# State-space scan at every fourth time in one sequence over all tiles, layer-1 keys behind the first output product, a one-array gate operand

## The chip, the cores and the metric

The kernel runs on one core of a Trainium2 chip. TensorE (PE) multiplies matrices, VectorE (DVE), ScalarE (ACT) and GpSimd (POOL) work on elements, and SyncE (SP) issues almost all DMA transfers; each engine takes its instructions in the order in which they were written. The metric is device time of one execution in microseconds (us).

## What is computed

Two decoder layers on 256 positions of width 4096. Each layer multiplies the normalised input by one wide matrix, runs a recurrent branch (a state-space model in layer 0, a gated linear recurrence in layer 1), attends to a fixed memory, gates both and multiplies by an output matrix.

```python
for i in range(2):
    hn = rmsnorm(h, pre_norm[i])
    u, gate, q, q_gate = split(hn @ w_in[i], [3072, 6144, 7168])
    y = s5_mixer(u, ...) if i == 0 else rglru_mixer(u, ...)
    m = memory_attention(q, rmsnorm(mem, mem_norm[i]), w_kv[i])   # k and v are mem_n @ w_kv
    h = h + rmsnorm(concat[y * silu(gate), m * silu(q_gate)] @ w_out[i], post_norm[i])

def s5_mixer(u, ...):      # 192 groups of 16 channels, 64 complex states each
    x = einsum(u, Bbar)                      # input of each state
    s[t] = Abar * s[t-1] + x[t]              # diagonal recurrence over 256 times
    y = gelu(re(einsum(s, C)) + d * u)
    return y * sigmoid(y @ w_glu + b_glu)
```

## The kernel before, in words

Activations lie with channels on the partitions and the 256 times along the free dimension. Every product splits its float32 operands in two parts, hi and lo: ACT rounds a weight piece to hi (L126), DVE subtracts to get lo (L90), and PE multiplies hi by both parts of the activation and lo by its hi part (L130). `add_phase` cuts each matrix into steps of one 512 KB weight piece, eight blocks of 128 by 128. There are 980 steps: u0 (96 steps), g0 (96), gq0, q0, k0, v0 and k1 (32 each) and glu (72), then out0 (128), v1 (32), u1 (96), gq1, q1, g1 with 12 gate steps, and out1. In form "w2" a block takes two matmuls, one of 512 columns and one of 256, in forms "n2", "n4" and "n8" three of 256.

`run` (L421) writes the program step by step. In a step come first the pieces of work that are due (`at`, `hook`), then the matmuls of the step, the split of the piece two steps ahead, then side work (`run_side`: generators that go on while a count of DVE and ACT time lies behind that of PE), and last the DMA of the piece five steps ahead into one of three `raw` buffers (`load_w`). All DMAs of `self.dma` (L134) go to the one SP queue, so a piece of side work stands in it between two weight pieces. The DMAs use eight completion semaphores in turn, and a DMA waits for the one issued eight before it.

The state-space branch `s5` is side work. `s5_a_b` forms the input coefficients and stores them in DRAM (`bD`). `x_load` (L818) fetches a tile's coefficients and two phases (even and odd times) of u, `x_mm` multiplies them, and the state input goes to a big buffer X. That buffer holds 48 of the 96 state tiles, so the branch runs in two blocks of 12 channel tiles: load, then 127 sequential scan steps of one DVE multiply and two adds, then the output stage. In that stage `y_coef` (L854) makes coefficients on POOL, `d0_mm` and `y_mm` multiply on PE, and DVE and ACT apply the GELU. The result goes to DRAM, rounded and remainder apart (`gHL`), and is read back as the operand of glu. A glu step may only be written when its tiles are done (`ready`); until then the steps written are without matmuls of weights.

`boundary` (L553) forms layer 1's input between out0 and u1, in 16 chunks c: f0 (a DVE multiply, then a DMA issued by POOL that adds x into the chunk `bh`), f1 two steps later (ACT writes `Bhn`, rounded) and f2 one step after (DVE writes the remainder).

Of the kernel before, what the change touches and what calls it, by code (L numbers as in the profile page):

```python
# [20 lines left out]
T = 256  # L21
# [7 lines left out]
BT = 48  # L29
TH = T // 2  # L30
# [15 lines left out]
def blocks(nm, form=None, n=0):  # L46
# [4 lines left out]
         "k0": blocks(KX, "n4", 4), "v0": [(0, KX, "v")], "k1": blocks(KX, "n4", 4),  # L51
         "glu": blocks(KE, "n4", 4), "out0": blocks(KD), "v1": [(0, KX, "v")],
         "u1": blocks(KE, "n4", 8), "gq1": blocks(KX), "q1": blocks(KX), "g1": blocks(KE), "out1": blocks(KD)}
# [9 lines left out]
class Trunk:  # L63
# [84 lines left out]
    def setup(self):  # L148
# [404 lines left out]
    def boundary(self):  # L553
        self.B = self.big.tile([128, 2, KD, T], F32R, name="Bhn", tag="B")
        rb = self.rbx.unsqueeze(1).to_broadcast([128, 2, T])
        for c in range(KD // 2):
# [32 lines left out]
            w = self.step + 1 + 2 * c  # L589
# [138 lines left out]

    def s5(self):
# [36 lines left out]
        yield  # L766
        self.mul(t0, nr, lr)
# [9 lines left out]
        self.mul(t0, kr, ar)  # L777
        self.mul(t1, nki, ai)
        self.add(k2r, t0, t1)
        self.mul(t0, nki, ar)  # L780
        self.mul(t1, kr, ai)
        self.sub(nk2i, t0, t1)
        yield
        self.mul(t0, ar, ar)
        self.mul(t1, ai, ai)
        self.sub(A2[:, :, 0, 0], t0, t1)
        self.sub(A2[:, :, 1, 1], t0, t1)
        yield
        self.mul(t0, ar, ai)
        self.ts(A2[:, :, 0, 1], t0, 2.0, ALU.mult)  # L790
        self.ts(A2[:, :, 1, 0], t0, -2.0, ALU.mult)
        d0s = [sp.tile([128, 128], F32, name=f"d0{i}", tag=f"d0{i}", bufs=1) for i in range(2)]
        W = [sp.tile([128, 1024], F32, name=f"W{i}", tag=f"W{i}", bufs=1) for i in range(2)] + [tail(2560, 1024)]
        W = [w.rearrange("p (i j c q) -> p i j c q", i=2, j=2, c=2) for w in W]
        for t in d0s + W:
            self.nc.gpsimd.memset(t, 0.0)
        yield
        asb = X0[:, 12288:12544].rearrange("p (k q) -> p k q", k=2)
        ps = self.ps_x.tile([128, 2, T], F32, name="psa", tag="x")
        for k in range(2):  # L800
            self.pe_t += 214
            self.nc.tensor.transpose(ps[:, k, 0:128], cf[:, 128 * k:128 * k + 128], self.ident)
        self.acopy(asb, ps[:, :, 0:128])
        yield "wait"
        for k, n, rows in ((0, 0, asb[0:NT, 0]), (1, 0, asb[NT:128, 0]), (1, 128 - NT, asb[0:2 * NT - 128, 1])):
            self.dma(self.aD[n:n + rows.shape[0], :, k], rows.rearrange("n (g q) -> n g q", g=2))
        yield "wait"
# [4 lines left out]
        self.ab = deque(self.s5_a_b(tail(0, 3072), 12, 6) + self.s5_a_b(tail(0, 3072), 18, 6))  # L812
        self.nc.gpsimd.memset(X[:, :, :, 0:1], 0.0)

        st = {}


        def x_load(ct, w, u):  # L818
# [10 lines left out]
        def x_mm(blk, ct):  # L829
            w, u, _ = st.pop(("x", ct))  # L830
            for i in range(2):
                ps = self.ps_x.tile([128, 2, 2, TH], F32, name="psx", tag="x")
                for j in range(2):
                    for c in range(2):
                        self.mm(ps[:, j, c, :], w[:, i, j, c, :], u[:, i, :], True, True, 218)
                n = 4 * ct - blk * BT + 2 * i
                self.acopy(X[:, n:n + 2, :, 1:], ps)


        v4 = lambda t: t.rearrange("p (c j m) -> p c j m", c=2, j=4)  # L840

        def y_load(ct, part):
            s = st.setdefault(ct, {})
            if part == 0:
                s["craw"] = v4(tail(1536 + 256 * (ct % 2), 256))
                self.dma(s["craw"], I["s5c"][ct])
            elif part == 1:
                s["b2"] = v4(tail(2048 + 256 * (ct % 2), 256))
                self.dma(s["b2"], I["s5b2"][ct])
            else:  # L850
                s["u"] = sp.tile([128, T], F32, name="u", tag="u")
                self.dma(s["u"], self.uF[ct])

        def y_coef(ct):  # L854
            s = st[ct]
            P = v4(tail(3584, 256))
            Q = v4(sp.tile([128, 256], F32, name="cQ", tag="cQ", bufs=1))
            g = self.nc.gpsimd
            for i, (re, im) in enumerate(((kr, nki), (k2r, nk2i))):
                C = v4(tail(2560 + 512 * (ct % 2) + 256 * i, 256))  # L860
                b = lambda v: v[:, 4 * ct:4 * ct + 4].unsqueeze(1).unsqueeze(3).to_broadcast([128, 2, 4, 32])
# [4 lines left out]
                s["C", i] = C  # L866

        def d0_mm(ct):
            s = st[ct]
            d = self.pm[:, 0, 0:32]  # L870
            for k in range(2):
                for j in range(4):
                    self.mm(d[32 * j:32 * j + 32], s["b2"][:, k, j, :], s["C", 0][:, k, j, :], k == 0, k == 1, 66)

        def d0_copy(ct):
            d = d0s[ct % 2]
            for j in range(4):
                r = slice(32 * j, 32 * j + 32)
                self.acopy(d[r, r], self.pm[r, 0, 0:32])

        def y_mm(blk, ct):
            s = st[ct]
            c = ct - blk * (BT // 4)
            ps = self.pm[:, 1, :].rearrange("p (e t) -> p e t", e=2)
            s["y"] = ps
            self.done.add(("ym", ct))
            ue = s["u"][:, 0:TH]
            self.mm(ps[:, 0, :], d0s[ct % 2], ue, True, False, 218)
            for e in range(2):
                for k in range(2):  # L890
                    for j in range(4):
                        self.mm(ps[32 * j:32 * j + 32, e, :], s["C", 1 - e][:, k, j, :],
                                X[:, c * 4 + j, k, e:e + TH], e == 1 and k == 0, k == 1, 74)

        def y_tasks(blk, ct, S):
# [25 lines left out]
            at(S - 5, lambda: y_load(ct, 0))
            at(S - 4, lambda: y_load(ct, 1))
            at(S - 2, lambda: y_coef(ct))
            at(S, lambda: y_load(ct, 2))
            at(S, lambda: d0_mm(ct))
            at(S + 1, lambda: d0_copy(ct))
            at(S + 2, lambda: y_mm(blk, ct))
# [484 lines left out]
```

## Time and profile before

| what | value |
|---|---|
| median of 3 runs | 3048.28 us (3039.66 to 3050.7) |
| profiled execution | 3042.13 us, of which the span from first to last instruction is 3040.4 us |
| PE busy | 2923.2 us, 96% of the span |
| DVE, ACT, POOL busy | 2084.3, 1586.9, 165.4 us |
| mean granted TensorE clock | 0.98 of full speed |

"Busy" is time in which an engine had an instruction running. Matmuls overlap one another, so their mean duration is longer than the distance from one to the next, and a row's count divided by its window gives the pace. A granted clock of 1.00 is 2.4 GHz, 0.50 is 1.2 GHz. Names left of an arrow are written, those right of it read.

### The profile page before, as it was taken

The numbers are of one execution on the slowest core, as the hardware profiler recorded it, in microseconds if no ns is written. First come the engines' busy times: TensorE is split into PE (matmuls) and PEld (weight loads), VectorE is DVE, ScalarE is ACT, GpSimd is POOL, SyncE is SP. The second block draws the span as 40 slices with busy tenths as digits, with TensorE's granted clock in tenths as the row PEclk, the third lists the DMA queues.
The fourth block names the chain that finished last, engine by engine and source line by source line (L and its number), as shares of the span: only waits on it lengthen the run. The fifth ranks groups of instructions, "written<-read, shape, count | busy, mean of one in ns | idle before, by whom it ended". The sixth has DMA issues, their size and how long they took to land.

```text
span 3040.4 us, 52558 instructions
## 1 busy us (share of the span) xinstructions
PE 2923.2 (96%) x18318; PEld 2582.6 (85%) x18318; DVE 2084.3 (69%) x4597; ACT 1586.9 (52%) x3073; POOL 165.4 (5%) x225
## 2 busy tenths in 40 slices
PE   9999999999999977999999998999999999999996
PEld 9998888888998976888888876988888888888885
DVE  8739989668999853565655555678888766655555
ACT  6444444454655443555655554456666555455553
POOL 1000000340000052000000001000000000000001
PEclk9999999999999987999999999999999999999998
DMA  8777666776767775656766689666667566666664
GB/s 273 217 215 223 199 197 201 214 228 207 244 214 233 217 237 184 211 188 215 239 208 198 202 237 242 196 211 216 214 209 218 188 217 196 198 205 202 200 205 156
DMA packets 286347, 644.12 MB, mean 212 GB/s; under 512 B 38912, under 2 KB 158976, under 8 KB 285824
## 3 DMA queue, kind: packets, MB, share of 16 engines
q1 hardware_dynamic: 279872, 634.72, 66.9%
q0 software_dynamic: 4352, 4.20, 0.9%
q8 instruction: 144, 2.36, 0.3%
q10 hardware_dynamic: 1856, 1.84, 0.2%
q14 instruction: 123, 1.01, 0.1%
HBM read 592.81 MB, written 47.81 MB: 211 GB/s over the span
## 4 chain that ended last, share of the span: by engine, by line
PE 80%; DMA 8%; DVE 6%; issue 2%; ACT 2%; SPq 1%; ACTq 0%; DVEq 0%; POOLq 0%
PE acc L130 76%; DVE lo L90 3%; DMA st<-gF 1%; PE pm L130 1%; DMA gHL<-gh 1%; PE psg L130 1%; PE psx L130 1%; ACT hi L126 1%; SPq L134 1%; DMA bh<-in_x 1%; DVE e L90 1%; DMA u<-uF 1%; DVE Bs L90 1%; DMA bo<-og 1%; DVE Bfin L90 0%
## 5 line engine op out<-in xcount | busy, mean ns | idle before, releaser
L90 DVE TENSOR_TENSOR lo<-raw,hi 128x512 fp32r<-128x512 f32 (+1 forms) x2434 | 1341.2, 587 | 773.3 <-ACT hi L126 734.5
L126 ACT CAST hi<-raw 128x512 fp32r<-128x512 f32 x1960 | 1139.9, 618 | 771.7 <-PE acc L130 358.4
L130 PE MATMUL acc<-A,hi 128*128 128x512 f32 (+1 forms) x4896 | 1494.6, 367 | 37.5 <-DMA A<-gHL 21.5
L130 PE MATMUL acc<-A,lo 128*128 128x256 f32 x4160 | 1175.5, 283 | 2.9 <-DVE lo L90 2.8
L130 PEld LDWEIGHTS acc<-A,hi 128*128 128x128 f32 x4896 | 886.1, 192 | 196.3 <-DMA A<-gHL 20.8
L130 PEld LDWEIGHTS acc<-A,lo 128*128 128x128 f32 x4160 | 796.0, 191 | 10.7 <-DVE lo L90 10.1
L130 PE MATMUL acc<-Bhn,hi 128*128 128x512 f32 (+1 forms) x2304 | 726.4, 373 | 13.2 <-ACT hi L126 13.2
L130 PE MATMUL acc<-Bhn,lo 128*128 128x256 f32 x2048 | 576.2, 281 | 2.5 <-DVE lo L90 2.5
L130 PEld LDWEIGHTS acc<-Bhn,hi 128*128 128x128 f32 x2304 | 419.7, 190 | 92.4 <-ACT hi L126 15.4
L130 PEld LDWEIGHTS acc<-Bhn,lo 128*128 128x128 f32 x2048 | 389.9, 190 | 5.8 <-DVE lo L90 5.5
L130 PE MATMUL acc<-Bmix,hi 128*128 128x512 f32 x1024 | 355.6, 391 | 0.4 <-ACT hi L126 0.4
L130 PE MATMUL acc<-Bmix,lo 128*128 128x256 f32 x1024 | 287.0, 280 | 0.2 <-DVE lo L90 0.2
L130 PEld LDWEIGHTS acc<-Bmix,hi 128*128 128x128 f32 x1024 | 191.5, 187 | 42.9 <-ACT hi L126 0.7
L130 PEld LDWEIGHTS acc<-Bmix,lo 128*128 128x128 f32 x1024 | 193.5, 189 | 0.8 <-DVE lo L90 0.8
L130 PE MATMUL acc<-hi,A 128*128 128x512 f32 x512 | 160.5, 395 | 12.6 <-ACT hi L126 12.6
L90 DVE TENSOR_TENSOR Bs<-Bs,m 128x96 f32<-128x96 f32 x508 | 168.3, 331 | 2.9
L130 PEld LDWEIGHTS acc<-hi,A 128*128 128x128 f32 x512 | 97.0, 191 | 34.2 <-ACT hi L126 14.3
L126 ACT COPY e<-acc 128x256 f32<-128x256 f32 x200 | 73.5, 368 | 75.6 <-PE acc L130 74.7
L130 PE MATMUL acc<-lo,A 128*128 128x512 f32 x256 | 101.4, 396 | 0.0
L122 ACT ACTIVATE e<-e 128x256 f32<-128x256 f32 x64 | 26.7, 418 | 138.2 <-DVE e L90 138.0
L90 DVE TENSOR_TENSOR m<-A,Bs 128x192 f32<-128x192 f32 x254 | 90.4, 356 | 8.9 <-ACT Bs L126 3.5
L90 DVE TENSOR_TENSOR e<-e,acc 128x256 f32<-128x256 f32 x200 | 79.5, 410 | 7.1 <-ACT e L126 7.1
(148 smaller groups left out, 1574.1 us busy)
## 6 DMA issues: line engine op xcount, KB each, us to landing
raw<-in_w_out SPq DMA_DIRECT2D x256, 512.0 KB, 4.1
raw<-in_w_u SPq DMA_DIRECT2D x192, 512.0 KB, 4.1
raw<-in_w_g SPq DMA_DIRECT2D x192, 512.0 KB, 3.9
raw<-in_w_glu SPq DMA_DIRECT2D x72, 512.0 KB, 4.2
raw<-in_w_gq SPq DMA_DIRECT2D x64, 512.0 KB, 4.4
raw<-in_w_q SPq DMA_DIRECT2D x64, 512.0 KB, 4.0
raw<-in_w_k SPq DMA_DIRECT2D x64, 512.0 KB, 4.2
raw<-in_w_v SPq DMA_DIRECT2D x64, 512.0 KB, 4.4
```

The costliest lines, as they stand in the source:

```text
L90: self.nc.vector.tensor_tensor(out=out, in0=a, in1=b, op=op)
L122: self.nc.scalar.activation(out=out, in_=a, func=f, **kw)
L126: self.nc.scalar.copy(out=out, in_=a)
L130: self.nc.tensor.matmul(out, lhsT=lhsT, rhs=rhs, start=start, stop=stop)
L134: self.nc.sync.dma_start(out=out, in_=in_)
```

## The change

The scan now steps over four times at once. X holds all 96 state tiles with 64 entries each (the state at every fourth time), so there is one sequence of 63 scan steps, on arrays twice as wide. For that the coefficients of three earlier phases are formed and stored (`bD[0]` to `bD[2]`), `x_load` fetches four phases, and the output stage uses four sets of output coefficients and three within-phase matrices. Output tiles are written three steps apart, before two and a half. k1 moves from ahead of glu to behind out0, and k1 and u1 use form w2 throughout. The boundary's chunks are written two and a half steps apart, before two. The glu operand is stored as one float32 array (`gF`), loaded in pairs of tiles and split on ACT and DVE (`g_turn`), where before both parts were stored and loaded.

```diff
-         "k0": blocks(KX, "n4", 4), "v0": [(0, KX, "v")], "k1": blocks(KX, "n4", 4),
+         "k0": blocks(KX, "n4", 4), "v0": [(0, KX, "v")], "k1": blocks(KX),
-         "u1": blocks(KE, "n4", 8), ...
+         "u1": blocks(KE), ...
@@ boundary
-            w = self.step + 1 + 2 * c
+            w = self.step + 1 + 5 * c // 2
@@ s5
-        for f in self.s5_a_b(X0[:, 4096:], 0, KE // 2):
-            yield f() if f else "wait"
+        for h in range(2):
+            for f in self.s5_a_b(X0[:, 4096:], h * KE // 2, KE // 2):
+                yield f() if f else "wait"
...
         def x_load(ct, w, u):
-            u = u.rearrange("p (i t) -> p i t", i=2)
-            src = self.uF[ct].rearrange("(i j c) (e t) -> j e c i t", i=2, j=2, e=2)
-            for e, b in enumerate((self.bD, I["s5b"])):
-                bv = b.rearrange("(i j c) t k q -> j t c i k q", i=2, j=2)
-                for j in range(2):
-                    r = slice(64 * j + 32 * e, 64 * j + 32 * e + 32)
-                    self.dma(w[r, :, j], bv[j, ct])
-                    self.dma(u[r], src[j, e])
+            u = u.rearrange("p (i t) -> p i t", i=4)
+            src = self.uF[ct].rearrange("(i c) (e t) -> e c i t", i=4, e=L4)
+            for e in range(L4):
+                b = I["s5bc"] if e == L4 - 1 else self.bD[e]
+                bv = b.rearrange("(i g c) t k q -> t g k c i q", i=4, g=2)
+                for g in range(2):
+                    r = slice(32 * e + 16 * g, 32 * e + 16 * g + 16)
+                    for k in range(2):
+                        self.dma(w[r, :, k, 64 * g:64 * g + 64], bv[ct, g, k])
+                self.dma(u[32 * e:32 * e + 32], src[e])
...
         def y_coef(ct):
-            for i, (re, im) in enumerate(((kr, nki), (k2r, nk2i))):
-                C = v4(tail(2560 + 512 * (ct % 2) + 256 * i, 256))
+            for i, (re, im) in enumerate(kc):
+                C = Cs[ct % 2][:, i]
                 g.tensor_tensor(out=P, in0=s["craw"], in1=b(re), op=ALU.mult)
                 g.tensor_tensor(out=Q, in0=s["craw"], in1=b(im), op=ALU.mult)
-                g.tensor_tensor(out=C[:, 0], in0=P[:, 0], in1=Q[:, 1], op=ALU.add)
-                g.tensor_tensor(out=C[:, 1], in0=Q[:, 0], in1=P[:, 1], op=ALU.subtract)
+                for h in range(2):
+                    r, c = slice(64 * h, 64 * h + 64), slice(16 * h, 16 * h + 16)
+                    g.tensor_tensor(out=C[r, 0, :, c], in0=P[r, 0], in1=Q[r, 1], op=ALU.add)
+                    g.tensor_tensor(out=C[r, 1, :, c], in0=Q[r, 0], in1=P[r, 1], op=ALU.subtract)
...
+            for i in range(3):
+                self.mm(ps[:, i:3, :], d[:, i, :], u[:, 0:3 - i, :], i == 0, False, 330 - 53 * i)
-            for e in range(2):
+            for e in range(L4):
+                o = e == L4 - 1
                 for k in range(2):
                     for j in range(4):
+                        self.mm(ps[32 * j:32 * j + 32, e, :], C[:, 0 if o else e + 1, k, j, :],
+                                X[:, ct * 4 + j, k, o:o + TQ], o and k == 0, e > 1 and k == 1, 60)
...
-            at(S - 2, lambda: y_coef(ct))
+            at(S - 4, lambda: y_coef(ct))
...
+        while z < KE:
+            if a < KE and a < z + 3 and ("u", a) in self.done:
+                x_load(a, wv[a % 3], us[a % 4])
+                a += 1
+            if a > z and st["x", z][2] <= self.step - 3:
+                x_mm(z)
+                z += 1
+            yield "wait"
+        for t in range(1, TQ):
+            sb = X[:, :, :, t:t + 1].to_broadcast([128, NT, 2, 2])
+            self.mul(m, A4, sb)
...
+            y_tasks(ct, S + 3 * ct)
@@ build
-        mark["k1"] = len(self.steps)
-        self.add_phase("k1", A, self.ev_row(self.kd[1], self.rbm))
         mark["glu"] = len(self.steps)
...
-        mark["v1"] = len(self.steps)
+        self.add_phase("k1", A, self.ev_row(self.kd[1], self.rbm))
         self.add_phase("v1", A, self.ev_v(self.vd[1], "st"))
```

The first place is the SP queue at a tile of the state input; `raw` is a weight piece, `uF` the stored u, and the other two names left of an arrow are buffers of coefficients and u. Before, between two weight pieces:

```order
L134 DMA raw<-in_w_u 128x1024
L134 DMA W_1815<-bD 32x2x256
L134 DMA Bs_370<-uF 32x2x128
L134 DMA W_1815<-bD 32x2x256
L134 DMA Bs_370<-uF 32x2x128
L134 DMA W_1815<-in_s5b 32x2x256
L134 DMA Bs_370<-uF 32x2x128
L134 DMA W_1815<-in_s5b 32x2x256
L134 DMA Bs_370<-uF 32x2x128
L134 DMA raw<-in_w_u 128x1024
```

The same queue in the changed kernel, again between two weight pieces:

```order
L134 DMA raw<-in_w_u 128x1024
L134 DMA Bs_369<-bD 16x4x64 x4
L134 DMA Bs_369<-uF 32x4x64
L134 DMA Bs_369<-bD 16x4x64 x4
L134 DMA Bs_369<-uF 32x4x64
L134 DMA Bs_369<-bD 16x4x64 x4
L134 DMA Bs_369<-uF 32x4x64
L134 DMA Bs_369<-in_s5bc 16x4x64 x4
L134 DMA Bs_369<-uF 32x4x64
L134 DMA raw<-in_w_u 128x1024
```

Eight transfers between two weight pieces have become twenty. All 24 tiles now stand in one run, from step 79 to step 109, three tiles in every four steps.

The second place is POOL in the output stage. Before, one set of coefficients and the start of the next; a tile has two sets:

```order
L862 TENSOR_TENSOR Bs_370<-Bs_370,cf 128x256
L863 TENSOR_TENSOR cQ<-Bs_370,cf 128x256
L864 TENSOR_TENSOR Bs_370<-Bs_370,cQ 128x128
L865 TENSOR_TENSOR Bs_370<-cQ,Bs_370 128x128
L862 TENSOR_TENSOR Bs_370<-Bs_370,cf 128x256
```

In the changed kernel, one set and the start of the next; a tile has four:

```order
L871 TENSOR_TENSOR Bs_369<-Bs_369,cf 128x128
L872 TENSOR_TENSOR Bs_369<-Bs_369,cf 128x128
L875 TENSOR_TENSOR C_2997<-Bs_369 64x4x16
L876 TENSOR_TENSOR C_2997<-Bs_369 64x4x16
L875 TENSOR_TENSOR C_2997<-Bs_369 64x4x16
L876 TENSOR_TENSOR C_2997<-Bs_369 64x4x16
L871 TENSOR_TENSOR Bs_369<-Bs_369,cf 128x128
```

A tile takes 24 instructions where it took 8, on arrays of half the width or less.

The third place is DVE in the boundary, two chunks of it: `bh<-bo` is f0, the pair of `Bhn` rows with the sum behind it is f2. Before:

```order
L90 TENSOR_TENSOR bh<-bo,rbx 128x512
L90 TENSOR_TENSOR lo<-raw,hi 128x512 x2
L103 SCALAR_TENSOR_TENSOR Bhn<-bh,sm,Bhn 128x256 x2
L90 TENSOR_TENSOR acc<-acc,bs 128x512
L90 TENSOR_TENSOR lo<-raw,hi 128x512 x2
L90 TENSOR_TENSOR bh<-bo,rbx 128x512
```

In the changed kernel, from one even chunk's f0 to the next even chunk's:

```order
L90 TENSOR_TENSOR bh<-bo,rbx 128x512
L90 TENSOR_TENSOR lo<-raw,hi 128x512 x2
L103 SCALAR_TENSOR_TENSOR Bhn<-bh,sm,Bhn 128x256 x2
L90 TENSOR_TENSOR acc<-acc,bs 128x512
L90 TENSOR_TENSOR lo<-raw,hi 128x512 x4
L103 SCALAR_TENSOR_TENSOR Bhn<-bh,sm,Bhn 128x256 x2
L90 TENSOR_TENSOR acc<-acc,bs 128x512
L90 TENSOR_TENSOR bh<-bo,rbx 128x512
```

Before, one chunk's f2 stood between two f0. Now two stand between an odd chunk's f0 (the first row) and the next even chunk's (the last).

## Rows read from the trace of the kernel before

**Rows 1.** The profile page: span, and PE's busy time, share and instructions.

```profile
span 3040.4 us, 52558 instructions
...
PE 2923.2 (96%) x18318; PEld 2582.6 (85%) x18318; DVE 2084.3 (69%) x4597; ACT 1586.9 (52%) x3073; POOL 165.4 (5%) x225
```

**Rows 2.** Busy time by stretch: length, PE, PEld, DVE, ACT, POOL, clock, DMA share, GB/s.

```profile
40.00:80.00 40.00, 40.00 (x336) 40.00 (x335) 33.72 (x84) 26.58 (x51) 0.00 (x0) 1.00 0.87 288
560.00:680.00 120.00, 111.94 (x1095) 97.40 (x1094) 69.72 (x109) 64.63 (x162) 63.50 (x95) 0.99 0.74 227
1080.00:1200.00 120.00, 85.17 (x913) 74.43 (x914) 48.15 (x82) 46.76 (x126) 49.95 (x80) 0.75 0.63 201
1520.00:1560.00 40.00, 40.00 (x233) 35.24 (x232) 21.22 (x35) 19.28 (x35) 0.00 (x0) 1.00 0.68 211
1800.00:1920.00 120.00, 98.67 (x566) 85.95 (x565) 67.85 (x127) 57.74 (x112) 15.59 (x13) 0.94 0.88 240
```

**Rows 3.** Timeline of SP, state input, block 0: start, duration, queue, line, transfer, count.

```profile
168.68 0.38 SPq L134 DMA_DIRECT2D W<-bD  x1
...
172.57 0.38 SPq L134 DMA_DIRECT2D raw<-in_w_u  x1
...
210.82 0.41 SPq L134 DMA_DIRECT2D W<-bD  x1
...
215.96 0.37 SPq L134 DMA_DIRECT2D raw<-in_w_u  x1
```

**Rows 4.** Timelines of SP and ACT at the coefficient loads; idle time in brackets.

```profile
133.17 4.50 SPq L134 DMA_DIRECT2D Bs<-aD  x8
138.11 0.35 SPq L134 DMA_DIRECT2D raw<-in_w_u  x1
...
144.31 1.14 ACT L126 CAST hi<-raw 128x512 fp32r<-128x512 f32 x2 [8.24 <-DMA raw<-in_w_u]
```

**Rows 5.** Timeline of PE, output stage of block 0: small products (counts of records).

```profile
604.37 0.38 PE L130 MATMUL pm<-u,d 128*128 128x128 f32 x2
604.69 1.08 PE L130 MATMUL pm<-Bs 128*32 128x128 f32 x32
...
608.63 1.95 PE L130 MATMUL psx<-acc,W 128*128 128x128 f32 x16
610.84 0.33 PE L130 MATMUL pm<-Bs 128*32 128x32 f32 x16 [0.27 <-issue]
```

**Rows 6.** POOL groups: shapes, count, busy us, mean ns; then two instructions of the timeline.

```profile
L862 POOL TENSOR_TENSOR Bs<-Bs,cf 128x256 f32<-128x256 f32 x48 | 34.4, 717 | 841.2 <-DMA Bs<-in_s5c 438.0 <-DMA W<-bD 397.7 <-DMA raw<-in_w_g 2.9
L864 POOL TENSOR_TENSOR Bs<-Bs,cQ 128x128 f32<-128x128 f32 x48 | 29.4, 612 | 42.7 <-PE pm L130 39.8
...
599.60 0.46 POOL L865 TENSOR_TENSOR Bs<-cQ,Bs 128x128 f32<-128x128 f32 x1
600.14 0.61 POOL L862 TENSOR_TENSOR Bs<-Bs,cf 128x256 f32<-128x256 f32 x1
```

**Rows 7.** Timelines of DVE and ACT in the boundary: f0, f0, f1, f0.

```profile
1810.01 0.68 DVE L90 TENSOR_TENSOR bh<-bo,rbx 128x512 f32<-128x512 f32 x1
1814.42 0.68 DVE L90 TENSOR_TENSOR bh<-bo,rbx 128x512 f32<-128x512 f32 x1
...
1820.32 0.91 ACT L122 ACTIVATE Bhn<-bh,sm 128x256 fp32r<-128x256 f32 x2 [7.27 <-DMA bh<-in_x]
...
1826.10 0.69 DVE L90 TENSOR_TENSOR bh<-bo,rbx 128x512 f32<-128x512 f32 x1
```

**Rows 8.** The costliest groups on the profile page: the two instructions of a scan step.

```profile
L90 DVE TENSOR_TENSOR Bs<-Bs,m 128x96 f32<-128x96 f32 x508 | 168.3, 331 | 2.9
...
L90 DVE TENSOR_TENSOR m<-A,Bs 128x192 f32<-128x192 f32 x254 | 90.4, 356 | 8.9 <-ACT Bs L126 3.5
```

More of the change, by code (lines that the diff above doesn't have):

```diff
@@ L28 @@
 NT = 96
-BT = 48
-TH = T // 2
+L4 = 4
+TQ = T // L4
 MAGIC = 12582912.0
@@ L776, in s5 @@
         yield
[L777 to L783, printed above, removed]
+        for (pr, pi), (qr, qi) in zip(kc, kc[1:]):
+            self.mul(t0, pr, ar)
+            self.mul(t1, pi, ai)
+            self.add(qr, t0, t1)
+            self.mul(t0, pi, ar)
+            self.mul(t1, pr, ai)
+            self.sub(qi, t0, t1)
+            yield
         self.mul(t0, ar, ar)
@@ L785, in s5 @@
         self.mul(t1, ai, ai)
-        self.sub(A2[:, :, 0, 0], t0, t1)
-        self.sub(A2[:, :, 1, 1], t0, t1)
+        self.sub(nr, t0, t1)
+        self.mul(t0, ar, ai)
+        self.ts(den, t0, 2.0, ALU.mult)
         yield
[L789 to L793, printed above, removed]
@@ L794, in s5 @@
-        W = [w.rearrange("p (i j c q) -> p i j c q", i=2, j=2, c=2) for w in W]
-        for t in d0s + W:
+        self.mul(t0, nr, nr)
+        self.mul(t1, den, den)
+        self.sub(A4[:, :, 0, 0], t0, t1)
+        self.sub(A4[:, :, 1, 1], t0, t1)
+        yield
+        self.mul(t0, nr, den)
+        self.ts(A4[:, :, 0, 1], t0, 2.0, ALU.mult)
+        self.ts(A4[:, :, 1, 0], t0, -2.0, ALU.mult)
+        W = [sp.tile([128, 1024], F32, name="W0", bufs=1), tail(0, 1024), tail(1024, 1024)]
+        for t in W:
@@ L796, in s5 @@
             self.nc.gpsimd.memset(t, 0.0)
         yield
[L798 to L806, printed above, removed]
@@ L827, in x_load, with x_mm @@
             st["x", ct] = (w, u, self.step)
-        def x_mm(blk, ct):
+        def x_mm(ct):
             w, u, _ = st.pop(("x", ct))
[L831 to L837, printed above, removed]
@@ L840, in s5 @@
-        v4 = lambda t: t.rearrange("p (c j m) -> p c j m", c=2, j=4)
+            ps = self.ps_x.tile([128, 4, 2, TQ], F32, name="psx", tag="x")
+            for i in range(4):
+                for k in range(2):
+                    self.mm(ps[:, i, k, :], w[:, i, k, :], u[:, i, :], True, True, 224)
+            self.acopy(X[:, 4 * ct:4 * ct + 4, :, 1:], ps)
+        v4 = lambda t, j=4: t.rearrange("p (c j m) -> p c j m", c=2, j=j)
+        Cb = [W[0], sp.tile([128, 1024], F32, name="C1", bufs=1)]
@@ L842, in y_load @@
+        Cs = [c.rearrange("p (s k j m) -> p s k j m", s=L4, k=2, j=4) for c in Cb]
+        D = [aux[:, 384 * i:384 * i + 384].rearrange("p (s m) -> p s m", s=3) for i in range(2)]
         def y_load(ct, part):
@@ L976, in s5 @@
+        self.pen = 120
+        self.nc.gpsimd.memset(aux, 0.0)
+        S = self.step + 7
+        for ct in range(KE):
+            y_tasks(ct, S + 3 * ct)
         while ("g", KE - 1) not in self.done:
@@ L985, in s5_a_b @@
         a5 = self.aD.rearrange("(t j) g k q -> j g t (k q)", j=4)
-        b5 = self.bD.rearrange("(j g c) t k (h q) -> j g h c t k q", j=4, g=2, h=2)
-        rows = [(j, g, slice(32 * j + 16 * g, 32 * j + 16 * g + 16)) for j in range(4) for g in range(2)]
         half = [slice(0, n // 2), slice(n // 2, n)]
@@ L1315, in build @@
         self.hook(mark["out0"] + 4, mem1)
-        self.hook(mark["k1"] + 8, lambda: self.done.add(("v", 0)))
+        self.hook(mark["glu"] + 6, lambda: self.done.add(("v", 0)))
         def att1_begin():
@@ L1386, in layout @@
     r["s5b2"] = b2.reshape(24, 128, 2, 4, 32)
[L1387 removed]
+    r["s5c"] = c.reshape(24, 128, 2, 4, 16)
     return r
```

219 lines of the change are left out of this document (92 added, 127 removed).

## The prediction

> **What bounds the kernel now.** I read the profile page first: PE is busy for 2923 of 3040 us [rows 1], so time is gained only where PE idles or runs at a lower clock, and any other queue costs time as soon as it makes PE wait. Then the busy time by stretch [rows 2]. In a plain stretch PE is busy without a gap and shows 233 matmuls in 40 us; a step of form w2 has 16, so it takes 40 / (233 / 16) = 2.75 us. A step of three matmuls per block has 24, and 336 in 40 us give 2.86 us. Three stretches lose time. The output stage of the first scan block (560 to 680 us) has 8 us of idle PE. That of the second (1080 to 1200) has 35 us, and its clock is 0.75 of full speed, the lower level of 1.2 GHz part of the time, which costs a further 0.25 x 85 = 21 us. The boundary (1800 to 1920) has 21 us, and 0.06 x 99 = 6 us by the clock. These are what the change can win: 65 us in the output stages, 27 in the boundary. DVE, which the shorter scan relieves, is busy for 69% and is not the bound. Last I read the timelines of the queues that the change fills more, SP, POOL and DVE in the boundary.
>
> **The state input, on SP.** A tile's x_load grows from 8 transfers to 20 and all 24 tiles stand in steps 79 to 109, so SP has 480 such transfers, 31 weight pieces and 8 others in 31 steps. In the trace, eight transfers and the way to the next weight piece take 172.57 - 168.68 = 3.89 us, 0.49 each, in a quick tile and 215.96 - 210.82 = 5.14 us, 0.64 each, in a slow one, where a transfer waits for the one eight before it to land [rows 3]. What a transfer carries hardly shows: weight pieces of 512 KB stand in the same rows with the same 0.4 us. That the weight pieces are behind this queue is seen at the coefficient loads: eight loads in one step hold SP from 133.17 to 138.11, the piece behind them comes late, and ACT idles for 8.24 us [rows 4].
>
> By the Trainium skill (DMA: Bandwidth & Descriptors, "Issuing engines are not separate DMA queues") the time to initiate a DMA is usually small beside the DMA itself. By that rule only the data would count here, and these are the same 384 KB per tile as before, so the term below would be nothing and the sum 3034. The trace does not agree for transfers of 16 KB: with 0.4 us each their issue fills the queue.
>
> PE needs for these steps 31 x 2.75 = 85 us, and 24 x 1.95 = 47 us for the products of the state input [rows 5], whose number stays: 132 us. Before, 8 transfers per tile fitted beside that; 20 don't. SP needs 480 x p + 39 x 0.49. At p = 0.49 that is 254 us, at 0.64 it is 326. I take 0.51, near the quick tile, because the waits come about once per weight piece and now spread over 20 transfers: 264 us. SP can be three weight buffers ahead at the start, 3 x 2.75 = 8 us. The term is 264 - 132 - 8 = **+124 us**, from +114 to +186. PE is then busy for half the time, and the clock will fall as it did in the second output stage; even at 1.2 GHz throughout PE would need twice 132, no more than SP, so I add nothing for it.
>
> **The output stage, on POOL.** Before, the small products of a tile take 0.38 + 1.08 + 0.33 = 1.8 us [rows 5], 24 tiles 43 us, and with the 65 us of lost time the stage costs 108 us beside its weight steps. Now the small products are 3 + 32 + 8 per tile. The narrow ones took 1.08 / 16 = 0.07 us at 128 columns and 0.33 / 8 = 0.04 at 32, so 40 of them take 1.6 to 2.7 us, I take 1.9; three wider ones take at most 0.38 each, I take 0.8. PE's pace is 3 x 2.75 + 2.7 = 10.9 us a tile. POOL has 24 instructions per tile, 8 of width 128 and 16 of width 64, which the trace does not show. Undisturbed, 256 columns take 0.61 us and 128 take 0.46; in the mean, with DVE at the same memory, 0.72 and 0.61 [rows 6]. Continued to 64 columns that is 0.385 or 0.56, and a tile takes 8 x 0.46 + 16 x 0.385 = 9.8 us or 8 x 0.61 + 16 x 0.56 = 13.9 us. I take 12.0, the middle, because POOL will run without a pause and DVE won't: longer than PE's 10.9. PE waits at the first small product of each tile, since a tile's coefficients can be made only one tile ahead. The stage takes 24 x 12 = 288 us, its 72 weight steps 198, so it costs 90 where it cost 108: **-18 us**, from -44 (PE's pace) to +28. The waits before glu go, since its operand is done 60 steps earlier; what takes their place is POOL.
>
> The Trainium skill (GPSIMD Engine Reference, "Elementwise — side-by-side cycle accounting") prices two-input work on GpSimd by the element, about 2.6 cycles at 1.2 GHz. By that a tile's 2048 columns would take an estimated 4.4 us, POOL would never be late, and the sum would be that of the rival in which POOL keeps up, 3132. The rows disagree: half the columns saved 0.15 us of 0.61, so most of an instruction's time does not go with its columns.
>
> **The boundary.** k1 puts 32 more steps before u1, enough for its 40 steps if it kept pace. It won't: f0 of a chunk at 1810.01 has its f1 at 1820.32, 10.3 us later, because the DMA behind it must land, and the next f0 on the same chain comes 5.8 us after that, for it stands on DVE behind parts that wait for ACT, which waits in f1 [rows 7]. Before, even and odd chunks were two such chains side by side, 16.1 us for 4 steps of 11.0. In the new order an even f0 stands behind the f2 of the odd chunk before it. So the chains become one: 4.4 us from even to odd f0, 10.3 to the odd f1, and about 4.6 to the next f0 (one step of casts less), 19.3 us for 5 steps of 13.7. Over 8 pairs and less 8 us of lead, 37 us are lost against 33 by the same reckoning for before, which lost 27 in fact. ACT and DVE also have k1's results to move in it. I take **+8 us**, from -27 (all covered) to +19.
>
> **The rest.** k1 and u1 in form w2: 48 steps x 0.11 = **-5**. Coefficient loads of eight transfers now stand in u0 twice instead of once: ACT's 8.24 us less two steps of lead is **+3**, 0 to +6. The scan: 63 steps on 66 weight steps. DVE's other work is 21.2 / 14.56 = 1.46 us per step [rows 2] and leaves 1.29. The three instructions took 0.356 + 2 x 0.331 = 1.02 us [rows 8] and are twice as wide; between 1.02 and 2.04 I take 1.35, nearer to the rows, as a third of a microsecond does not go with width there: 63 x 0.06 = **+4**, 0 to +47. DVE's 127 us or more of saved scan lie beside a busy PE and count nothing. The glu operand's split (12 casts, 12 subtractions) lies beside v0, where DVE has room; without that cover it is some 15 us. The layer-1 memory normalised once less is off the path too.
>
> Sum: 124 - 18 + 8 - 5 + 3 + 4 = +116. Against the profiled execution's own 3042 us that is **3158 us**. The median of the runs is 6 us higher, 0.2%, which I leave inside the range.
>
> **Rivals.**
> - *POOL keeps up.* If a 64-column instruction takes much less than the line through the rows says, or the two halves of the partitions run beside each other, the output stage goes at PE's 10.9 us: 26 us less, 3132. For it: half the partitions, and the idle POOL of before. Against it: 24 instructions where 8 were.
> - *The transfers' landing sets the pace of SP.* At 0.64 us each the state input costs 186 instead of 124: 3220; with POOL at 13.9 us, 3266. For it: the slow tile, and three times as many separate pieces of memory to move. Against it: small transfers land sooner than a weight piece.
> - *Issue goes with bytes, and the state input hides.* A transfer of 16 KB would hold SP for a part of what 64 KB do; then the first term is gone and the time is 3158 - 124 = 3034, no slower than before. It decides below 480 p + 19 = 148, p = 0.27 us. Against it: the quick tile's transfers, of 64 and 32 KB in turn, follow each other at one distance of 0.49 us, and a weight piece of 512 KB holds SP no longer.
>
> **How the numbers follow.** My forecast has 0.50 (3110 to 3205), POOL keeping up 0.22, slow landing 0.18, a hidden state input 0.10. Adding the low bounds of the first three terms (3158 - 10 - 26 - 35) gives 3087, slow landing with a slow POOL 3266; the range is 3085 to 3270. A measurement of this kernel can tell 0.5%, some 15 us, from no change. All cases but the last are slower by more than that; the last lies within it or, with POOL keeping up, beyond it: faster 0.04, same 0.06, slower 0.90.
>
> **What will show it.** Right: from about 230 to 495 us PE is busy for about half the time, SP's transfers follow each other every 0.5 us without a wait for weight buffers, and ACT waits over 100 us for `raw` pieces; in the output stage POOL is busy throughout and PE waits for it; no wait for glu's operand; pairs of chunks in the boundary 17 to 20 us apart. Wrong: a busy PE while the state input loads (first term), or PE steps of 2.75 us with POOL idle between tiles (second).

## The result and the profile after

The changed kernel takes 3156.62 us in the median of 4 runs (3151.57 to 3163.31), the kernel before beside it 3043.97: a ratio of 1.0373, 95% interval 1.0337 to 1.0408. It is slower, by what was forecast (3158). The profiled execution took 3151.57 us.

Page of the changed kernel, its span and busy times (before: [rows 1]):

```profile
span 3149.8 us, 52556 instructions
...
PE 2992.3 (95%) x18798; PEld 2616.5 (83%) x18798; DVE 1964.9 (62%) x3559; ACT 1577.4 (50%) x3017; POOL 297.7 (9%) x609
```

Its busy time by stretch, columns as in [rows 2]: coefficient stage, state input, scan, output stage, a plain stretch, boundary.

```profile
100.00:200.00 100.00, 93.24 (x646) 87.22 (x644) 72.16 (x155) 34.93 (x62) 0.00 (x0) 0.95 0.81 216
200.00:232.00 32.00, 27.52 (x147) 23.45 (x146) 29.66 (x47) 13.11 (x24) 0.00 (x0) 0.95 0.81 257
232.00:515.00 283.00, 218.74 (x1008) 192.31 (x1008) 64.71 (x110) 62.43 (x116) 2.30 (x3) 0.75 0.41 116
515.00:700.00 185.00, 182.16 (x1023) 155.88 (x1023) 172.96 (x349) 80.77 (x159) 0.00 (x0) 1.00 0.62 187
700.00:1000.00 300.00, 288.17 (x3259) 242.79 (x3258) 189.75 (x303) 159.77 (x370) 262.37 (x577) 0.99 0.64 192
1000.00:1240.00 240.00, 240.00 (x1531) 215.84 (x1530) 148.76 (x258) 134.83 (x243) 0.00 (x0) 1.00 0.74 230
1800.00:1960.00 160.00, 141.36 (x672) 116.68 (x671) 98.25 (x183) 77.87 (x153) 19.33 (x16) 0.94 0.85 239
```

The loss stands in the third row: 64 us of idle PE, and a granted clock of 0.75 over 219 busy us, which costs 0.25 x 219 = 55 more. DVE, ACT and POOL are mostly idle there, and the DMA engines are less busy than anywhere else (0.41, and 116 GB/s where a plain stretch has 230). What is busy is SP. Its timeline there, one tile and the two weight pieces behind it (before: [rows 3]):

```profile
329.98 1.98 SPq L134 DMA_DIRECT2D Bs<-bD  x4
332.01 0.42 SPq L134 DMA_DIRECT2D Bs<-uF  x1
332.47 1.95 SPq L134 DMA_DIRECT2D Bs<-bD  x4
334.46 0.42 SPq L134 DMA_DIRECT2D Bs<-uF  x1
...
337.27 1.83 SPq L134 DMA_DIRECT2D Bs<-in_s5bc  x4
339.15 0.42 SPq L134 DMA_DIRECT2D Bs<-uF  x1
339.68 0.85 SPq L134 DMA_DIRECT2D raw<-in_w_u  x2
```

SP issues without a gap, 9.6 us for twenty transfers; the next tile, in which some of them wait, takes 11.2. The waits of the changed kernel between 232 and 515 us show who stands behind it (sum, number, longest):

```profile
ACT hi L126 <- DMA raw<-in_w_u: 106.8, 17, 9.6
ACT hi L126 <- DMA raw<-in_w_g: 102.7, 12, 9.5
...
PE psx L130 <- DMA Bs<-uF: 55.4, 19, 6.0
```

ACT waits for weight pieces queued behind a tile; PE waits also for the last transfer of a tile itself. The products of the state input (tile view: shortest, median, longest ns, first and last start):

```profile
L130 PE MATMUL psx<-Bs x256: 275/421/448, 265.5 to 510.1; 128*128 128x64 f32 x128
L130 PE MATMUL psx<-Bs,W x128: 275/282/444, 255.2 to 488.2; 128*128 128x64 f32 x128
```

24 tiles have 23 distances: (510.1 - 255.2) / 23 = 11.1 us a tile, where PE needs 5.5 (1.29 steps of 2.75 us and 1.95 us of products).

### The profile page after: what moved, and what is told of

Read it like the earlier page. It is cut to its first block, busy times and chain, and to the rows that moved or that the text cites. A ratio compares the mean times of both kernels' runs of the same rounds, so it can differ in the third digit from the quotient of the medians.

```text
span 3149.8 us, 52556 instructions
## 1 busy us (share of the span) xinstructions
PE 2992.3 (95%) x18798; PEld 2616.5 (83%) x18798; DVE 1964.9 (62%) x3559; ACT 1577.4 (50%) x3017; POOL 297.7 (9%) x609
## 4 chain that ended last, share of the span: by engine, by line
PE 71%; DMA 8%; POOL 7%; SPq 5%; DVE 5%; issue 3%; ACT 1%; ACTq 0%; POOLq 0%; DVEq 0%
PE acc L130 68%; SPq L134 5%; DVE lo L90 2%; DMA raw<-in_w_u 2%; POOL Bs L871 1%; POOL Bs L872 1%; POOL C L875 1%; DMA raw<-in_w_g 1%; POOL W L876 1%; PE psg L130 1%; POOL W L875 1%; POOL C L876 1%; DMA st<-gF 1%; DMA uF<-e 1%; ACT hi L126 1%
## 5 line engine op out<-in xcount | busy, mean ns | idle before, releaser
L90 DVE TENSOR_TENSOR lo<-raw,hi 128x512 fp32r<-128x512 f32 x1960 | 1310.9, 695 | 1035.4 <-ACT hi L126 1015.4
L130 PE MATMUL acc<-A,hi 128*128 128x512 f32 (+1 forms) x4768 | 1524.3, 377 | 30.2 <-ACT hi L126 22.7
L130 PE MATMUL acc<-A,lo 128*128 128x256 f32 x4160 | 1187.5, 285 | 5.3 <-DVE lo L90 5.1
L130 PEld LDWEIGHTS acc<-A,lo 128*128 128x128 f32 x4160 | 809.8, 195 | 13.8 <-DVE lo L90 12.9
L130 PE MATMUL acc<-Bhn,hi 128*128 128x512 f32 x2048 | 722.2, 397 | 4.6 <-ACT hi L126 4.6
L130 PEld LDWEIGHTS acc<-Bhn,hi 128*128 128x128 f32 x2048 | 385.6, 188 | 95.3 <-ACT hi L126 6.4
L130 PE MATMUL acc<-hi,A 128*128 128x512 f32 x512 | 161.5, 397 | 11.1 <-ACT hi L126 11.1
L629 POOL TENSOR_TENSOR Bfin<-Bfin 128x1024 f32<-128x1024 f32 x4 | 10.3, 2589 | 1196.1 <-DVE Bfin L90 1196.1
L563 POOL DMA_DIRECT2D bh<-in_x x16 | 19.3, 1208 | 921.0 <-ACT hi L126 810.2
L130 PE MATMUL psx<-Bs 128*128 128x64 f32 x256 | 50.5, 380 | 48.7 <-DMA Bs<-uF 41.7
```

The source lines that it names most:

```text
L90: self.nc.vector.tensor_tensor(out=out, in0=a, in1=b, op=op)
L130: self.nc.tensor.matmul(out, lhsT=lhsT, rhs=rhs, start=start, stop=stop)
L563: self.nc.gpsimd.dma_start(out=h, in_=self.I["x"][2 * c:2 * c + 2].rearrange("k p t -> p k t"), accum_op=ALU.add)
L629: self.nc.gpsimd.tensor_tensor(out=o, in0=o, in1=h, op=ALU.add)
```

## The experiments

"Against the changed kernel" is the difference of the two ratios to before, times 3044 us; each is uncertain by some 12 to 14 us, so e3 and e11 can't be told from no change.

| run | median us | ratio to before (95%) | against the changed kernel |
|---|---|---|---|
| changed kernel | 3156.62 | 1.0373 (1.0337 to 1.0408) | |
| e1: 12 transfers a tile | 3107.04 | 1.0206 (1.0180 to 1.0232) | -51 |
| e2: 9 transfers a tile | 3084.74 | 1.0138 (1.0108 to 1.0167) | -72 |
| e3: quarter of the bytes | 3148.95 | 1.0338 (1.0314 to 1.0362) | -11 |
| e4: two queues | 3100.22 | 1.0183 (1.0161 to 1.0204) | -58 |
| e5: 20 transfers, spread | 3038.67 | 0.9991 (0.9974 to 1.0009) | -116 |
| e6: 9 transfers, spread | 3050.06 | 1.0016 (1.0003 to 1.0029) | -109 |
| e7: boundary, later f1 | 3122.51 | 1.0257 (1.0239 to 1.0275) | -35 |
| e8: less on POOL | 3133.23 | 1.0289 (1.0271 to 1.0307) | -26 |
| e9: before, 20 transfers | 3167.79 | 1.0399 (1.0374 to 1.0424) | |
| e10: before, later f1 | 3021.91 | 0.9922 (0.9905 to 0.9939) | |
| e11: boundary, two steps | 3148.65 | 1.0339 (1.0323 to 1.0355) | -10 |
| e12: e5, e7 and e8 | 2990.69 | 0.9823 (0.9809 to 0.9838) | -167 |

**e1, merged coefficients.**

```diff
...
-                    for k in range(2):
-                        self.dma(w[r, :, k, 64 * g:64 * g + 64], bv[ct, g, k])
+                    self.dma(w[r, :, :, 64 * g:64 * g + 64].rearrange("p i k q -> p (i k) q"),
+                             b[ct, 16 * g:16 * g + 16].rearrange("c i (k q) -> c (i k) q", k=2))
...
```

> The changed kernel with the coefficients in DRAM in such an order that one transfer brings both their parts: 12 transfers per tile of the state input (8 of 16 x 8 x 64, 4 of u) in place of 20, the same 384 KB and the same runs of 256 bytes; storing the coefficients takes 24 transfers in place of 6. Theory (SP's time goes with the number of transfers): the changed kernel needs 11.1 us from tile to tile in its state input; eight transfers less at 0.49 us leave 7.2, so SP needs 24 x 7.2 = 172 us where PE needs 132 and SP has a lead of 8; the loss falls from 129 us to some 32, and the time from 3152 to 3055 (3040 to 3070). Rival (landing: the bytes and runs set the pace): the time stays at 3152, within 10.

Half the expected gain. A transfer moves its data in runs, pieces of contiguous memory, here of 256 bytes: 64 in a transfer of coefficients, 128 in one of u, and in e1 128 in both. The timeline of SP in e1 says why the gain is short:

```profile
343.58 1.21 SPq L134 DMA_DIRECT2D Bs<-bD  x2
344.83 0.59 SPq L134 DMA_DIRECT2D Bs<-uF  x1
```

A transfer of coefficients with twice the runs holds SP for 0.60 us, not 0.49, and the transfers of u, unchanged, now take 0.59 where they took 0.42. Both theories failed in size: the time fell, but not with the number alone.

**e2, nine transfers.**

```diff
...
+            for i in range(4):
+                self.dma(self.uX[m, :, :, i].rearrange("e c t -> c e t"),
+                         u[32 * i:32 * i + 32].rearrange("p (e t) -> p e t", e=L4))
...
+            self.dma(u, self.uX[ct].rearrange("e c i t -> (e c) i t"))
...
```

> As the run with merged coefficients, and u stored a second time, phase by phase, when it is formed (four more transfers per tile, beside u0), so that one transfer brings a tile's u: 9 transfers per tile in the state input. Theory (number): 24 x (11.1 - 11 x 0.49) = 137 us on SP, no more than PE's 132 with the lead of 8; the state input hides and the time is 3152 - 125 = 3027 (3015 to 3045), a little faster than before the change. Rival (landing): 3152, or later still, since 96 transfers of short runs are added.

SP in e2:

```profile
296.78 3.78 SPq L134 DMA_DIRECT2D Bs<-bD  x6
300.60 1.24 SPq L134 DMA_DIRECT2D Bs<-in_s5bx  x2
```

A gain of 72 us where 125 was expected. Again 0.62 us for the larger ones, 5.6 a tile; tiles stand 7.6 us apart, still more than PE's 5.5, because the weight pieces and the four added stores of u, some 0.47 us each, stand in the same queue. The added stores of coefficients and u also cost (PE in 100 to 200 us: 86.5, the changed kernel 93.2).

**e3, a quarter of the bytes.**

```diff
-                        self.dma(w[r, :, k, 64 * g:64 * g + 64], bv[ct, g, k])
-                self.dma(u[32 * e:32 * e + 32], src[e])
+                        self.dma(w[r, 0:1, k, 64 * g:64 * g + 64], bv[ct, g, k][:, 0:1])
+                self.dma(u[32 * e:32 * e + 32, 0:1], src[e][:, 0:1])
...
```

> The changed kernel with all its 20 transfers per tile, but each brings a quarter of its rows (the state input is left incomplete): 96 KB per tile in place of 384, and a quarter of the separate runs. Theory (number): nothing changes but the waits for a transfer eight before, some 0.03 to 0.05 us of the 0.52 per transfer: 3130 to 3152. Rival (landing, bytes): the state input takes a quarter to a half of its time, hides beside PE, and the time is 3020 to 3040.

SP in e3, and a window of its state input:

```profile
351.23 1.76 SPq L134 DMA_DIRECT2D Bs<-bD  x4
353.03 0.42 SPq L134 DMA_DIRECT2D Bs<-uF  x1
```

```profile
300.00:340.00 40.00, 29.27 (x130) 25.36 (x129) 6.47 (x10) 7.91 (x15) 0.00 (x0) 0.72 0.25 71
```

The rates of issue and of PE stay (130 matmuls in 40 us, in the changed kernel 136), though the DMA engines move 71 GB/s, not 97. A transfer of coefficients of 16 runs holds SP for 0.42 us in the median, as one of 64 runs does in the changed kernel: there the number of transfers is what counts. Landing and bytes are excluded as the main cause; the 11 us are not clear of the noise.

**e4, half the coefficients issued by ACT.**

```diff
+                        q = self.nc.scalar if g else self.nc.sync
+                        q.dma_start(out=w[r, :, k, 64 * g:64 * g + 64], in_=bv[ct, g, k])
```

> The changed kernel with 8 of the 16 coefficient transfers per tile issued by ACT, the other 12 transfers by SP: the same transfers and bytes. Theory (each issue holds the engine that issues it): SP needs 172 us as with merged coefficients; ACT has 2 casts per step and the 24 copies, 62 us, and 192 issues at 0.49 us, 94: 156 us, beside PE's 132. The time is 3050 to 3075. Rival (the issue, or the landing, is a resource that both queues share): 3152, within 10; rival (ACT's issue waits in order behind buffers that come free late): ACT's casts come later and the gain is less than half, 3100 or more.

Moving eight issues off SP gained 58 us, so the issue is not one resource that both queues share; but the gain is less than half of the loss, as the last rival said. ACT in e4:

```profile
333.93 4.52 ACTq L835 DMA_DIRECT2D Bs<-bD  x4
...
339.45 0.37 ACT L126 COPY e<-acc 128x256 f32<-128x256 f32 x1 [5.19 <-DMA Bs<-bD]
```

ACT stands 5.19 us behind its own transfers before it can go on. The Trainium skill (DMA: Bandwidth & Descriptors, "Issuing engines are not separate DMA queues") says that a second issuing engine saves only the time of initiating, usually small beside the DMA itself. Here it was not small: eight of twenty issues moved were worth 58 us.

**e5, the same twenty transfers, spread.**

```diff
...
-            if a < KE and a < z + 3 and ("u", a) in self.done:
-                x_load(a, wv[a % 3], us[a % 4])
-                a += 1
+            while a < 4 * KE and self.step >= x0 + 15 * a // 16 and a // 4 < z + 3 and ("u", a // 4) in self.done:
+                x_load(a // 4, wv[a // 4 % 3], us[a // 4 % 4], a % 4)
+                a += 1
...
```

> The changed kernel with the same 20 transfers per tile, but spread out: five transfers (one phase) at a time, a tile in 3.75 steps in place of 1.29, so the state input ends at step 168 in place of 109, the scan and the output stage follow later and still end before glu. Nothing else differs. Theory (SP's number of transfers bounds, at 0.46 us each in the changed kernel's trace): SP needs 20 x 0.46 + 3.75 x 0.5 = 11.1 us per tile, PE 3.75 x 2.75 + 1.95 = 12.3; the loss of 129 us hides, 3020 to 3040. Rival (small transfers slow the weight pieces wherever they stand, or the lower clock of a stretch with small gaps costs by itself): 3080 or more.

The state input of e5:

```profile
232.00:560.00 328.00, 323.91 (x1975) 285.11 (x1974) 157.15 (x273) 138.55 (x264) 2.32 (x3) 1.00 0.72 200
```

4 us of idle PE at full clock. The loss is a matter of when the transfers stand in SP's queue, and it takes the clock's loss with it.

**e6, nine transfers, spread** (e2 with a tile in 2.5 steps).

```diff
...
+            while a < 4 * KE and self.step >= x0 + 5 * a // 8 and a // 4 < z + 3 and ("u", a // 4) in self.done:
...
```

> As the run with 9 transfers per tile, spread to a tile in 2.5 steps. In that run SP needed 7.6 us per tile and PE 1.29 x 2.75 + 1.95 = 5.5; at 2.5 steps PE needs 8.8 and SP 6.3. Theory (number): the state input hides; what stays is the idle time in the coefficient stage, which the 18 further stores there brought (7 us more between 100 and 200 us), so 3030 to 3045, behind the spread of 20 transfers. Rival (the loss of the run with 9 transfers stood in the clock, not in SP): 3070 or more.

Slower than e5 by some 8 us (7 of uncertainty), as expected, and 5 us beyond the range: fewer transfers buy nothing once they are spread. Their preparation costs: between 100 and 232 us PE is busy for 112.6 us, in e5 for 122.4.

**e7, f1 later.**

```diff
-            self.at(w + 2, f1)
-            self.at(w + 3, f2)
+            self.at(w + 4, f1)
+            self.at(w + 5, f2)
```

> The changed kernel with f1 of a boundary chunk four steps behind f0 in place of two, and f2 five in place of three. Theory (f1 stands on ACT ahead of the casts and waits for the accumulating transfer, which lands some 8 us after its issue; two steps are 5.5 us): four steps are 11 us and cover it; ACT doesn't wait for bh, the 18 us per pair of chunks become 13.7, and 25 to 30 us go: 3122 to 3130. Rival (the transfers themselves, three per chunk and 512 KB of weights per step, bound the boundary): 3140 or more.

In the changed kernel's boundary (before: [rows 7]) f0 of an even chunk, of the odd one and of the next even one on DVE, then on ACT f1 of the even chunk and of the odd one. Behind them stand ACT's waits for `bh` in the whole kernel (sum, number, longest):

```profile
1839.79 0.68 DVE L90 TENSOR_TENSOR bh<-bo,rbx 128x512 f32<-128x512 f32 x1
1843.59 0.68 DVE L90 TENSOR_TENSOR bh<-bo,rbx 128x512 f32<-128x512 f32 x1
1857.28 0.68 DVE L90 TENSOR_TENSOR bh<-bo,rbx 128x512 f32<-128x512 f32 x1
...
1848.33 0.91 ACT L122 ACTIVATE Bhn<-bh,sm 128x256 fp32r<-128x256 f32 x2 [6.36 <-DMA bh<-in_x]
...
1852.70 0.91 ACT L122 ACTIVATE Bhn<-bh,sm 128x256 fp32r<-128x256 f32 x2 [0.87 <-DMA bh<-in_x]
```

```profile
ACT Bhn L122 <- DMA bh<-in_x: 46.0, 10, 6.9
```

In e7 that wait is gone from the list, and PE has no gap left:

```profile
1800.00:1960.00 160.00, 160.00 (x815) 136.11 (x814) 119.94 (x246) 91.24 (x175) 19.34 (x16) 1.00 0.93 275
```

So the boundary's loss was ACT's wait for the accumulating transfer.

**e8, one of four coefficient sets on DVE.**

```diff
...
+                g = self.nc.vector if i == 3 else self.nc.gpsimd
...
```

> The changed kernel with one of a tile's four sets of output coefficients made by DVE, so POOL has 18 instructions per tile in place of 24. In the changed kernel's output stage a tile takes 11.65 us, POOL is busy for 92% and PE waits 0.4 us per tile for it. Theory (POOL bounds the stage, PE close behind): POOL needs 8.7 us per tile, PE's own pace remains, and 24 x 0.4 = 10 us go: 3137 to 3147. Rival (POOL doesn't bound): 3152, or later by what six more instructions on DVE hold up, up to 15 us.

The copies of `psd`, one set per tile, in the changed kernel and in e8:

```profile
L126 ACT COPY aux<-psd x96: 212/230/236, 724.5 to 994.5; 32x96 f32<-32x96 f32 x96
```

```profile
L126 ACT COPY aux<-psd x96: 210/231/237, 722.9 to 978.2; 32x96 f32<-32x96 f32 x96
```

(994.5 - 724.5) / 23 = 11.74 us a tile became 11.10, 15 us in all; the runs gave 26, more than expected, but with an uncertainty of 12. In the changed kernel PE waits for POOL; in e8 it has almost no gap left in the stage:

```profile
PE psd L130 <- POOL C L875: 8.7, 12, 2.0
```

```profile
700.00:1000.00 300.00, 298.96 (x3436) 257.53 (x3436) 233.88 (x475) 171.77 (x402) 207.89 (x433) 1.00 0.66 205
```

So POOL did bound the stage, and 11.1 us is the pace of PE.

**e9, twenty transfers in the kernel before.**

```diff
-                    self.dma(w[r, :, j], bv[j, ct])
+                    for i in range(2):
+                        for k in range(2):
+                            self.dma(w[r, i, j, k], bv[j, ct][:, i, k])
```

> The kernel before with each of its four coefficient transfers per tile split in four: 20 transfers per tile, the same data, nothing else changed. Theory (number of transfers on SP): in the first block a tile of the state input takes 60.4 / 11 = 5.5 us in the trace of before; at the 11.1 us of the changed kernel 12 tiles lose 67 less 8 of lead, 59. In the second block tiles stand 10.9 us apart, between output tiles; there SP needs 20 x 0.46 for them, and about 4 for weights, loads and stores, so 0 to 27 are lost. 3100 to 3130. Rival (what costs in the changed kernel is its order, all tiles in one run beside the last u0 steps): no change.

The products of the state input in e9, the first two rows block 0, the third block 1:

```profile
L130 PE MATMUL psx<-Bs,W x128: 275/421/553, 177.7 to 287.4; 128*128 128x128 f32 x128
L130 PE MATMUL psx<-Bs x64: 275/384/550, 197.5 to 295.9; 128*128 128x128 f32 x64
...
L130 PE MATMUL psx<-acc,W x192: 270/275/275, 651.5 to 820.4; 128*128 128x128 f32 x192
```

Twenty transfers a tile make the kernel before as slow as the changed one, without its order of tiles. (The runs of coefficients are halved too, from 1 KB to 512 bytes; by e3 that counts for little.) The time is 38 us beyond the range. Block 0 has 10.7 us a tile, about as expected; block 1 has (820.4 - 651.5) / 11 = 15.4 where I had allowed 13.2, so 49 us are lost there and not 0 to 27. With some 58 in block 0 that is 107 of the 123 us; where the rest stands was not traced.

**e10, f1 later in the kernel before** (the edit of e7).

> The kernel before with f1 four steps behind f0 and f2 five, k1 where it was and chunks two steps apart. Before lost 27 us in the boundary. Theory (the loss is ACT's wait for the accumulating transfer): 20 to 27 us go without k1's move, 3016 to 3025; k1's place is worth nothing by itself. Rival (two steps per chunk are too few for the chunks' work, 16 chunks need the 64 steps that k1's move gives): less than 10 us, 3033 or more.

22 us faster than before, as the theory said: k1's move is not needed to hide the boundary. ACT's wait for `bh`, 52.6 us in the kernel before, is gone here too.

**e11, chunks two steps apart.**

```diff
-            w = self.step + 1 + 5 * c // 2
+            w = self.step + 1 + 2 * c
```

> The changed kernel with boundary chunks two steps apart, as before the change. The prediction's reckoning: even and odd chunks are two chains again, 16.1 us per pair against 11.0 that PE needs, 8 x 5.1 less 8 of lead is 33; the changed kernel's 18 us against 13.7 is 34 less 8. So 3150 to 3165. If the merged chain is what holds it (my reason for the +8), it should be 5 to 10 us faster instead, 3142 to 3147.

The even chunks' f0 in e11, the second and the last of eight:

```profile
1813.02 0.69 DVE L90 TENSOR_TENSOR bh<-bo,rbx 128x512 f32<-128x512 f32 x1
...
1901.53 0.69 DVE L90 TENSOR_TENSOR bh<-bo,rbx 128x512 f32<-128x512 f32 x1
```

These are six pairs, 14.75 us each against PE's 11.0, 30 us over eight pairs; the changed kernel's pairs lie 17.9 apart against 13.7, 34 us. By the distances the merged chain costs some 4 us. The time lies between what the two theories said, and the runs can't tell them apart: they put the difference at 10 us with an uncertainty of 12.

**e12, e5, e7 and e8 together.**

> The changed kernel with the three single edits together: state input spread over 3.75 steps a tile (measured -113 us), boundary f1 four steps behind f0 (-30), one of four coefficient sets on DVE (-19). They stand in three different stretches; summed, 3152 - 162 = 2990. In the spread kernel the output stage lies beside the normalising of mem, which also uses DVE, so the last may bring less: 2985 to 3005, faster than both kernels.

```profile
PE 2915.7 (98%) x18798; PEld 2553.8 (85%) x18798; DVE 1992.6 (67%) x3703; ACT 1572.9 (53%) x3018; POOL 245.5 (8%) x465
```

1.8% faster than the kernel before, as expected: the change pays once its three queues are relieved. Not all of that is the change's own, as the later f1 also helps the kernel before (e10). Against e10 the gain is 30 us of the 53. Which part of the change brings it was not tried.

## Why the prediction was right, step by step

- **State input, +124: measured 119** (64 idle, 55 clock), and e5 takes 116 away. The pace was 24 x 11.1 = 266 us, reckoned 264, and SP set it: e3 leaves it as it is with a quarter of the bytes, e5 hides it, e9 brings it into the kernel before. That the clock adds nothing beyond SP's pace fits, as in e5 both parts go together; it was not tested apart. PE was busy for 77% of the stretch and not for half, since the lower clock makes its work longer. That "what a transfer carries hardly shows" holds from 16 to 64 runs (e3) and fails in e1 and e2. Landing as the pace of SP, and issue by bytes, are excluded by e3. The border of that last rival is mis-added: PE's 132 us and 8 of lead are 140, not 148, so p = 0.25; nothing hangs on it.
- **Output stage, -18: -24.** At 11.74 us a tile it costs 24 x 11.74 - 198 = 84 us, where 12.0, the middle of two bounds, was taken. POOL bounded it, but closer to PE than reckoned: 64 columns took 0.32 us undisturbed, where the line through the rows gave 0.385, and 0.43 in the mean; PE's own pace was 11.1 (e8), not 10.9. The estimate of 4.4 us a tile from the Trainium skill's price by the element (GPSIMD Engine Reference, "Elementwise — side-by-side cycle accounting") is not borne out: POOL's rows from 700 to 1010 us sum to 272.5 / 24 = 11.4.
- **Boundary, +8: about 0.** 18.6 us idle and 0.06 x 141 by the clock are 27, as before. The chain is the one described, with smaller terms: in the rows of e7's section 3.8 us from even to odd f0, 9.1 to the odd f1 and 4.6 to the next f0, and the pairs are 17.9 us apart in the mean, not 19.3.
- **Coefficient loads, +3: +13**, outside its range. PE lost 11.2 us and 6 by the clock from 100 to 232 us; the kernel before lost 4.4 there. I counted the eight loads at the 4.50 us of [rows 4]; here they take nearly twice as long (8.55 us, the second time 8.38), and ACT waits 10.69 us. SP and ACT in the changed kernel:

```profile
138.39 8.55 SPq L134 DMA_DIRECT2D Bs<-aD  x8
```

```profile
153.39 3.67 ACT L126 CAST hi<-raw 128x512 fp32r<-128x512 f32 x6 [10.69 <-DMA raw<-in_w_u]
```

- **Scan, +4: about +3,** from a wrong size. A scan step takes 0.556 + 2 x 0.513 = 1.58 us, not 1.35: twice the width of [rows 8] costs about half as much again, not a third. DVE groups of the changed kernel, 515 to 700 us:

```profile
L90 DVE TENSOR_TENSOR lo<-raw,hi 128x512 fp32r<-128x512 f32 x124 | 84.7, 685 | 10.5 <-ACT hi L126 10.0 <-PE acc L130 0.4
L90 DVE TENSOR_TENSOR Bs<-Bs,aux 128x192 f32<-128x192 f32 x118 | 60.5, 513 | 0.0
L90 DVE TENSOR_TENSOR aux<-aux,Bs 128x384 f32<-128x384 f32 x59 | 32.8, 556 | 1.0
```

  124 subtractions are 62 steps in 185 us, 2.98 each, 14 us lost at 2.75. But the first scan of before, which I had as free, was not: 428 half subtractions, 107 steps, from 235 to 540 us are 2.85 each, 11 us.
- No wait for glu's operand, as said: glu's weight pieces are loaded from 1178.7 us on, and PE is busy for all of 1000 to 1240. The kernel before waited there for `gHL`, 21.5 us.

119 - 24 + 0 + 13 + 3 - 5 (forms, not measured apart) = 106 us of the 109 between the two profiled executions. The main term was right, by its mechanism and to 5 us. That the whole +116 came so near is partly luck: the other terms missed by -6, -8, +10 and -1 us, to both sides.

## What to carry over

Count transfers per step on the queue that also feeds the weights, before counting bytes: twenty small ones in one step starved PE while the DMA engines were 41% busy, and the same twenty, five at a time over 3.75 steps, cost almost nothing (e5). An instruction that waits for a transfer belongs as many steps behind its issue as the transfer takes, or everything behind it in its engine waits along (e7, e10).

## What was not expected of the hardware

- The time that a transfer holds SP does not go with its own runs alone. In the median it is 0.42 us in the changed kernel, with 64 runs (coefficients) and with 128 (u) alike, and 0.42 with a quarter of these in e3. In e1, where all transfers have 128 runs, it is 0.57 to 0.59, for the unchanged ones of u too, and in e2 0.60 for the coefficients. In the rows of e1 and e2 that is about 205 to 213 runs per us. This suggests a least time per transfer and, behind it, a rate of the whole queue: the 1536 runs of a tile would take an estimated 7.4 us at that rate, less than the 9.6 us of twenty transfers in the changed kernel, and about what twelve take in e1. It was not measured by itself.
- The eight loads of `aD` took 4.50 us in one kernel and 8.55 in the other with one shape; why was not tried.
- POOL in the changed kernel takes 0.32 us for 64 columns where DVE is idle, and 0.86 to 0.87 where a DVE subtraction of `lo` begins at the same time. That is seen in these rows and was not tried by itself. POOL, then DVE:

```profile
844.85 0.87 POOL L875 TENSOR_TENSOR C<-Bs 64x64 f32<-64x64 f32 x1
...
846.25 0.86 POOL L875 TENSOR_TENSOR C<-Bs 64x64 f32<-64x64 f32 x1
...
849.68 0.32 POOL L876 TENSOR_TENSOR C<-Bs 64x64 f32<-64x64 f32 x1
```

```profile
844.86 0.69 DVE L90 TENSOR_TENSOR lo<-raw,hi 128x512 fp32r<-128x512 f32 x1 [0.69 <-ACT hi L126]
...
846.24 0.69 DVE L90 TENSOR_TENSOR lo<-raw,hi 128x512 fp32r<-128x512 f32 x1 [0.23 <-ACT hi L126]
```
